# Five pairs of gates as seven block products, a hand-written ScalarE order at the border, and an earlier split of the next weights, in a bidirectional DeltaNet encoder layer

## The chip, the core and the metric

The program runs on one core of a Trainium2 chip. TensorE multiplies matrices (PE in the profile, PEld its weight loads), VectorE (DVE) and ScalarE (ACT) work on tiles, GpSimd (POOL) does small things, and SyncE's queue (SP) issues the DMAs. The metric is the device time of one execution in microseconds; 2003.53 us is the median of three runs before the change.

## What is computed

One encoder layer over 1040 positions (16 learned tokens and 1024 of the sequence), width 1024, all in float32. A normed input is projected into q, k, v, z, two sets of scalars, three parts of a short convolution and two gates:

```python
h = rmsnorm(h_res, norm1_w[l])
proj = h @ w_in[l]
(q, k, v, z, b_raw, a_raw, sc_b, sc_c, sc_x, gate_a, gate_b) = jnp.split(proj, SPLIT_POINTS, axis=-1)
o_dn = gated_deltanet_bidir(q, k, v, z, b_raw, a_raw, dn_conv_w[l], A_log[l], dt_bias[l], dn_norm_w[l])
y_a = o_dn @ w_branch_dn[l]
y_b = (sc_b * depthwise_conv_centred(sc_c * sc_x, sc_conv_w[l])) @ w_branch_sc[l]
merged = jax.nn.sigmoid(gate_a) * y_a + jax.nn.sigmoid(gate_b) * y_b
h_res = h_res + merged @ w_out[l]
...
gu = h2 @ w_gate_up[l]
h_res = h_res + (jax.nn.silu(gu[..., :D_FF]) * gu[..., D_FF:]) @ w_down[l]
```

The DeltaNet has 8 heads; each runs a scan over chunks forwards and one backwards, after the inverse of a triangular matrix for each chunk.

## The kernel before

**Precision.** Each dense product is made of three: weights and inputs are split into a high part (a cast on ACT, to `fp32r`) and a low part (the rest, a subtraction on DVE), and high·high, high·low and low·high are added in PSUM. So a weight block of 128 columns (a unit) against 512 positions is 8 x 3 = 24 matmuls of 512 columns, and its weights cost a DMA of 512 KB, a cast `wh` and a subtraction `wl`.

**Phase one** (the loop at L1377) works through units: three for each head (q, k, v: `u_qkv`) and fill units. Beside them run generators for each head: decay, norms and k·k products (`g_norm`, L603 to L642), the inverse (`g_inv`), the scan (`g_scan`, L816 to L953). The order of all engines is the program's own here (`manual_schedule`): a planner counts estimated times for PE, DVE and ACT in `T`, gives a generator a turn after each product when its due time has passed (`run_streams`), and lets queued DVE work go when DVE would be idle (`pump`). `pick` takes the next unit, head units first, and issues its DMA. The fill units are 24 of the short convolution (8 x three, `u_short`; the second of three is multiplied out of PSUM by DVE at L437), 8 gates (`u_gate`: for GH = 4 columns blocks, A and B; a tanh on ACT and a DMA) and 5 of z (`u_z`: a tanh on ACT, a multiplication on DVE, a DMA). Gates and z stand first (L965). The weights of the next unit are split by halves in four parts, at products 33, 36, 39 and 42 of the current unit (`SPL`, L1371), in the order high, low, high, low (`split_part`, L993 on ACT and L990 on DVE). A head's output is transposed on PE, copied by ACT into its own tile `NP` (L951) and written to `o_d`.

**The border** (L1483 to L1605) follows. Three z blocks are left (z0, z1, z2 in `z_rows`: for each half 24 matmuls, a tanh into `sz`, then a DVE multiplication). The four blocks of both gates that are left go in pairs: gates A and B of one column block are made by `pair` with seven block products instead of eight (`product`: 12 matmuls of 512 columns each): A11·B11, A12·B21, S2·T2, S1·T1, S3·T3, S4·B22, A22·T4. The moving blocks T1 to T4 are sums of blocks of the input, made once by `moving_sums` (subtractions and additions of 128x2048 on DVE, then `split`). The stationary blocks are sums of weight blocks for each pair (`pair_weights`, `sums`, `stationary2`). In `pair`, A11·B11 is put in the PSUM tile `bank`, ACT copies it to `o1`, and S2·T2 is added to the same `bank`. In the border DVE and PE keep the order of the text, and the other engines are ordered by the scheduler; after the first pair all are.

**Tiles.** `wh` and `wl` have two buffers each. Raw weights have two slots in phase one, and two more from L1482 on, in memory (`tp`) that phase one's tiles give back. PSUM has three kinds of bank in the profile: pm (2), pe (3), pd (3). After the border come the two branch products, the merge and the feed-forward; they are as before.

Of the kernel before, what the change touches and what calls it, by code (L numbers as in the profile page):

```python
# [16 lines left out]
P = 128  # L17
# [7 lines left out]
H = 8  # L25
# [1 line left out]
FF = 2816  # L27
NF = FF // P
ZH = 5
GH = 4  # L30
EPS = 1e-6
NEG = -1e30

# [15 lines left out]
def encoder_layer(ctx: ExitStack, tc: tile.TileContext, x, meta, norm1_w, w_in, w_ba,  # L49
                  dn_conv_w, A_log, dt_bias, dn_norm_w, sc_conv_w, w_bdn, w_bsc,  # L50
                  w_out, norm2_w, w_gu, w_down, final_w, out):
    nc = tc.nc
# [222 lines left out]
    def V(n, kind=0):  # L275
        return on("dve", (68 + 1.042 * n, 130 + 1.042 * n, 130 + 0.52 * n)[kind])

    def A(n):
        return on("act", 144 + 0.834 * n)
# [505 lines left out]
    def g_scan(h, st_):  # L785
# [74 lines left out]
        for i in range(NC):  # L860
# [12 lines left out]
            for d in act_:  # L873
# [4 lines left out]
                t = V(P, 1)  # L878
# [64 lines left out]
            yield T["pe"] + 300  # L943
        yield T["dve"] + HOP
        for c4 in range(2):
            oT = NP[:, 4 * c4:4 * c4 + 4, 1 - c4]
            pt = newbank()
            for c in range(4):
                transpose(pt[:, c], oacc[4 * c4 + c])
            yield pe(430)  # L950
            nc.scalar.copy(oT, pt)  # L951
            A(512)
            nc.sync.dma_start(o_d[h][:, c4 * 512:(c4 + 1) * 512].rearrange("p (c t) -> p c t", c=4), oT)  # L953
# [8 lines left out]
    fill_units += [(off + j * P, lambda w, j=j, d_=d_[j]: u_gate(j, d_, w), None, None)  # L962
                   for j in range(GH) for off, d_ in ((OGA, ta_d), (OGB, tb_d))]
    fill_units += [(OZ + h * P, lambda w, h=h: u_z(h, w), None, None) for h in range(ZH)]
    fill_units = fill_units[24:] + fill_units[:24]  # L965
    done = freed = 0
    decs, norms, invs, scans = [], [], [], []

# [16 lines left out]

    def split_part(u, i):
        u[3][0] = i + 1
        k = slice(4 * (i // 2), 4 * (i // 2) + 4)
        if i % 2:
            nc.vector.tensor_tensor(out=u[1][1][:, k], in0=u[2][:, k], in1=u[1][0][:, k].bitcast(F32), op=ALU.subtract)  # L990
            V(512)
        else:
            nc.scalar.copy(u[1][0][:, k], u[2][:, k])  # L993
            A(512)

    def start_streams():
        nonlocal ndec, nnorm, ninv, nscan
# [370 lines left out]
                yield T["act"]  # L1368

    dn = ph1.enter_context(tc.tile_pool(name="dn", bufs=1))  # L1370
    SPL = (33, 36, 39, 42)  # L1371
    for g in (gen0, gen1):
        for _ in g:
            pass
# [2 lines left out]
    while done < H or qkv_units or fill_units or any(ahead):  # L1377
        u = ahead.pop(0)
        if u is None:
            run_streams()  # L1380
            pump()
            T["pe"] += 100
            ahead.append(pick())
            continue
        for k in range(u[3][0], 4):
            split_part(u, k)
        if ahead[0]:
            ahead[0][1] = wtiles([P, KT, P])
        ahead.append(pick())
        for n_, _ in enumerate(u[0][1](u[1])):  # L1390
            if ahead[0] and n_ in SPL:
                split_part(ahead[0], SPL.index(n_))
            run_streams()
            pump()
    ph1.close()
# [46 lines left out]
    def moving_sums():  # L1442

        c = [slice(C0 + META + 512 * i, C0 + META + 512 * i + 512) for i in range(2)]
        f = lambda m: m.bitcast(F32)
        h0, h1 = ([f(hx[0][:, 4 * i:4 * i + 4, cc]) for cc in c] for i in range(2))
        l0, l1, l2 = ([f(t[:, :, cc]) for cc in c] for t in low_tiles)
        for i in range(2):
            for j in range(2):
                mov[f"B{i + 1}{j + 1}"] = hx[0][:, 4 * i:4 * i + 4, c[j]], [hx[1][4 * i + k][:, c[j]] for k in range(4)]  # L1450
        for i, n in enumerate(("T1", "T2", "T3")):
            t = big(f"b{i}", [P, 2, 4, 512])
            mov[n] = t[:, 0], t[:, 1]
        x, y = (big(g, [P, 2, 4, 512], F32) for g in ("mA", "b3"))
        t1, t2, t3, d_ = x[:, 0], x[:, 1], y[:, 0], y[:, 1]
        a, b = slice(0, 2), slice(2, 4)
        sub(t1, h0[1], h0[0])
        sub(d_, l0[1], l0[0])
        add(t1, t1, d_)
        split(*mov["T1"], t1)  # L1460
        yield
        sub(t2, h1[1], t1)
        add(t2[:, a], t2[:, a], l1[1])
        add(t2[:, b], t2[:, b], l2[1])
        split(*mov["T2"], t2)
        yield
        sub(t3, h1[1], h0[1])
        sub(d_[:, a], l1[1], l0[1][:, a])
        sub(d_[:, b], l2[1], l0[1][:, b])
        add(t3, t3, d_)  # L1470
        split(*mov["T3"], t3)
        yield
        t = big("b3", [P, 2, 4, 512])
        mov["T4"] = t[:, 0], t[:, 1]
        sub(t1, h1[0], t2)
        add(t1[:, a], t1[:, a], l1[0])
        add(t1[:, b], t1[:, b], l2[0])
        split(*mov["T4"], t1)
        yield

    raw_slots.extend((tp, f"raw{i}") for i in range(2))
    left, right = slice(0, 512), slice(512, 1024)  # L1482
    border0 = ExitStack()  # L1483
    border0.enter_context(tc.manual_schedule(engines={mybir.EngineType.DVE, mybir.EngineType.PE}))
    z_units = [wload(w_in, unit(OZ + ZH * P))]

    def z_rows(h):
# [93 lines left out]

    sums_of_blocks = moving_sums()
    z0, z1, z2 = (z_rows(h) for h in range(ZH, H))
    next(sums_of_blocks)
    z_units.append(wload(w_in, unit(OZ + (ZH + 1) * P)))
    next(z0)
    next(z0)
    next(sums_of_blocks)
    z_units.append(wload(w_in, unit(OZ + (H - 1) * P)))
    next(z0)  # L1590
    pair0 = pair_weights(0, GH)
    next(z1)
    pair0[1]()
    next(z1)
    pair0[2]()
    next(z1)
    next(z2)
    next(sums_of_blocks)
    next(z2)
    next(sums_of_blocks)  # L1600
    next(z2)
    for n, j in enumerate(range(GH, KT)):
        o1 = pair(n, j, *(pair_weights(n, j) if n else pair0))
        if n == 0:
            border0.close()  # L1605
# [370 lines left out]
```

## Time and profile before

| | |
|---|---|
| median of three runs | 2003.53 us (2002.02 to 2005.52) |
| the profiled execution | 2004.27 us, of it 2002.5 us from first to last instruction |
| phase one ends, z0 begins | 970.2 us |
| the first pair begins | 1009.3 us |
| TensorE matmul busy, DVE busy, ACT busy | 99%, 70%, 42% of the span |

A line of the waits names who waited, its line, for whom, then the microseconds in all, how many times, and the longest. A row of the timeline has the start in us, the length, the engine and line, what is written and read, how many, and in brackets the idle time before it and what ended it. Matmuls overlap: the length of one is no step, the distance between two starts is. A row of the windows has for each engine the busy time and the count, then the granted TensorE clock (1.00 is full), the busy share of the DMA engines and GB/s.

### The profile page before, as it was taken

The numbers are of one execution on the slowest core, as the hardware profiler recorded it, in microseconds if no ns is written. First come the engines' busy times: TensorE is split into PE (matmuls) and PEld (weight loads), VectorE is DVE, ScalarE is ACT, GpSimd is POOL, SyncE is SP. The second block draws the span as 40 slices with busy tenths as digits, with TensorE's granted clock in tenths as the row PEclk, the third lists the DMA queues.
The fourth block names the chain that finished last, engine by engine and source line by source line (L and its number), as shares of the span: only waits on it lengthen the run. The fifth ranks groups of instructions, "written<-read, shape, count | busy, mean of one in ns | idle before, by whom it ended". The sixth has DMA issues, their size and how long they took to land.

```text
span 2002.5 us, 31873 instructions
## 1 busy us (share of the span) xinstructions
PE 1977.3 (99%) x12011; PEld 1724.1 (86%) x12011; DVE 1396.6 (70%) x3013; ACT 836.4 (42%) x1961; POOL 107.8 (5%) x407
## 2 busy tenths in 40 slices
PE   9999999999999999999999999999999999999998
PEld 8998889899999999999788888887878888888887
DVE  6887688878888888855685544469766666656575
ACT  6472465536463646333244221225323333334344
POOL 2011101010101010100000000000000000000000
PEclk9999999999999999999999999999999999999999
DMA  3123222222132222221236743123765345477654
GB/s 132 65 90 95 80 80 75 85 61 83 45 99 59 75 59 75 59 65 43 95 116 242 249 160 95 63 93 110 256 217 217 123 155 188 158 273 244 195 172 167
DMA packets 131121, 251.00 MB, mean 125 GB/s; under 512 B 45013, under 2 KB 54662, under 8 KB 128535
## 3 DMA queue, kind: packets, MB, share of 16 engines
q1 hardware_dynamic: 130391, 247.92, 37.5%
q8 instruction: 94, 1.54, 0.3%
q10 hardware_dynamic: 576, 1.05, 0.1%
q14 instruction: 60, 0.49, 0.1%
HBM read 180.67 MB, written 68.25 MB: 124 GB/s over the span
## 4 chain that ended last, share of the span: by engine, by line
PE 90%; DVE 4%; DMA 3%; ACT 1%; issue 1%; SPq 0%; DVEq 0%; ACTq 0%
PE pm L341 33%; PE pd L1440 12%; PE pe L1440 5%; PE pm L1440 3%; PE pd L903 1%; PE pd L882 1%; PE pd L866 1%; PE pe L136 1%; PE pe L134 1%; PE pd L869 1%; PE pe L135 1%; PE pe L603 1%; PE pd L134 1%; PE pd L136 1%; PE pd L135 1%; PE pe L1882 1%
## 5 line engine op out<-in xcount | busy, mean ns | idle before, releaser
L341 PE MATMUL pm<-hTh,wh 128*128 128x512 f32 (+4 forms) x1296 | 446.4, 350 | 0.3 <-ACT hTh L1103 0.2
L341 PE MATMUL pm<-al,wh 128*128 128x512 f32 (+4 forms) x1296 | 445.9, 349 | 0.0
L341 PE MATMUL pm<-hTh,wl 128*128 128x512 f32 (+4 forms) x1296 | 443.8, 348 | 0.0
L341 PEld LDWEIGHTS pm<-hTh,wh 128*128 128x128 f32 x1296 | 242.7, 188 | 13.7 <-issue 0.8
L341 PEld LDWEIGHTS pm<-hTh,wl 128*128 128x128 f32 x1296 | 242.9, 188 | 12.3 <-issue 0.4
L341 PEld LDWEIGHTS pm<-al,wh 128*128 128x128 f32 x1296 | 242.9, 188 | 12.2 <-issue 0.4
L102 DVE TENSOR_TENSOR al<-raw,ring_h 128x1024 fp32r<-128x1024 f32 x73 | 88.6, 1222 | 65.0 <-ACT ring_h L101 64.7
L101 ACT CAST ring_h<-raw 128x1024 fp32r<-128x1024 f32 x73 | 76.7, 1053 | 107.8 <-PE pd L1884 34.4
L990 DVE TENSOR_TENSOR wl<-raw,wh 128x512 fp32r<-128x512 f32 x118 | 79.5, 688 | 30.6 <-ACT wh L993 30.2
L363 DVE SCALAR_TENSOR_TENSOR kq<-ra,wc,kq 128x520 f32<-128x520 f32 x128 | 96.6, 755 | 4.8 <-ACT kq L393 3.5
L889 ACT ACTIVATE w<-pd,small 128x128 f32<-128x128 f32 x128 | 39.9, 363 | 117.1 <-PE pd L882 116.7
L101 ACT CAST wh<-raw 128x1024 fp32r<-128x1024 f32 x47 | 49.3, 1050 | 87.4 <-PE pe L135 25.5
L496 DVE TENSOR_TENSOR tm<-fP,fN 128x135 f32<-128x135 f32 (+23 forms) x248 | 72.0, 290 | 4.9
L500 DVE TENSOR_TENSOR fP<-fP,tm 128x135 f32<-128x135 f32 (+23 forms) x248 | 71.6, 289 | 5.1
L993 ACT CAST wh<-raw 128x512 fp32r<-128x512 f32 x118 | 69.2, 621 | 3.7 <-issue 3.6
L1409 DVE TENSOR_TENSOR b<-pd,b 128x512 f32<-128x512 f32 x22 | 15.2, 690 | 69.4 <-PE pd L1440 69.4
L1819 ACT ACTIVATE b<-b 128x512 f32<-128x512 f32 x22 | 13.9, 632 | 114.3 <-DVE b L1409 114.3
L102 DVE TENSOR_TENSOR wl<-raw,wh 128x1024 fp32r<-128x1024 f32 x47 | 57.3, 1219 | 3.8 <-ACT wh L101 3.7
L856 ACT ACTIVATE jk<-NP 128x128 f32<-128x128 f32 x64 | 19.9, 311 | 83.5 <-DVE NP L852 82.5
L876 DVE SCALAR_TENSOR_TENSOR r<-pd,negEG,vS 128x128 f32<-128x128 f32 x120 | 36.8, 345 | 25.7 <-PE pd L866 25.2
L1440 PE MATMUL pd<-b_hl,wh 128*128 128x512 f32 x176 | 54.5, 391 | 0.0
L912 DVE SCALAR_TENSOR_TENSOR S<-S,eGl,pd 128x128 f32<-128x128 f32 x104 | 31.6, 342 | 30.2 <-PE pd L899 29.8
(590 smaller groups left out, 4689.5 us busy)
## 6 DMA issues: line engine op xcount, KB each, us to landing
raw<-in_w_in_dram SPq DMA_DIRECT2D x72, 512.0 KB
raw<-in_w_gate_up_dram SPq DMA_DIRECT2D x44, 512.0 KB
sums<-in_w_down_dram SPq DMA_DIRECT2D x22, 512.0 KB
t_d<-sums SPq DMA_DIRECT2D x11, 1024.0 KB
raw<-s_d SPq DMA_DIRECT2D x44, 256.0 KB
raw<-t_d SPq DMA_DIRECT2D x44, 256.0 KB
act_d<-b SPq DMA_DIRECT2D x43, 256.0 KB
raw<-act_d SPq DMA_DIRECT2D x33, 256.0 KB
```

Of the source, the lines that this page charges most:

```text
L101: nc.scalar.copy(hi, src)
L102: nc.vector.tensor_tensor(out=lo, in0=src, in1=hi.bitcast(F32), op=ALU.subtract)
L134: mm(po[:m, :n], wh[:, k, :m], xhk[:, t0:t0 + n], start=(k == 0), stop=False)
L135: mm(po[:m, :n], wh[:, k, :m], xlk[:, t0:t0 + n], start=False, stop=False)
L136: mm(po[:m, :n], wl[:, k, :m], xhk[:, t0:t0 + n], start=False, stop=(k == KT - 1))
L341: mm(po[:, :n], ww[:, k], f(k)[:, t0:t0 + n], start=i == 0, stop=i == 3 * KT - 1)
L363: nc.vector.scalar_tensor_tensor(out=acc, in0=raw[:, h0 + t:h0 + t + hn], scalar=wc[:, t, col:col + 1], in1=acc, op0=ALU.mult, op1=ALU.add)
L496: nc.vector.tensor_tensor(out=tv, in0=fP[:, 0:r, j:j + 1].broadcast_to([P, r, n]), in1=fN[:, j:j + 1, j + 1:32].broadcast_to([P, r, n]), o ...
L500: nc.vector.tensor_tensor(out=fP[:, 0:r, j + 1:32], in0=fP[:, 0:r, j + 1:32], in1=tv, op=ALU.subtract)
L990: nc.vector.tensor_tensor(out=u[1][1][:, k], in0=u[2][:, k], in1=u[1][0][:, k].bitcast(F32), op=ALU.subtract)
L993: nc.scalar.copy(u[1][0][:, k], u[2][:, k])
L1440: mm(po, x[:, k], y, start=k + i == 0 and not add_to, stop=k == 3 and i == 2, skip_group_check=add_to)
```

## The change

`GH` goes from 4 to 3: six gate units stay in phase one, and five pairs are made at the border. Of the fill units three gates come first, then the 24 of the short convolution, then three gates and five z. A head's output is copied into the tile of its values, `vS`, which the scan has done with, in place of `NP`. `split_part` casts both halves first, at products 24 and 27, and each low part follows from product 30 on when the planner takes its cast for done, at the latest from 44 on. At the border ACT too keeps the order of the text. There z1's weights are loaded before the first sum, `moving_sums` has its high and low parts in steps of their own, and z2's and the pair's steps stand in another order around them.

```diff
-GH = 4
+GH = 3
...
-            oT = NP[:, 4 * c4:4 * c4 + 4, 1 - c4]
+            oT = vS[:, 4 * c4:4 * c4 + 4]
...
-    fill_units = fill_units[24:] + fill_units[:24]
+    fill_units = fill_units[24:24 + 3] + fill_units[:24] + fill_units[24 + 3:]
...
-        k = slice(4 * (i // 2), 4 * (i // 2) + 4)
-        if i % 2:
+        k = slice(4 * (i % 2), 4 * (i % 2) + 4)
+        if i >= 2:
             nc.vector.tensor_tensor(out=u[1][1][:, k], in0=u[2][:, k], in1=u[1][0][:, k].bitcast(F32), op=ALU.subtract)
+            on("dve", 0, u[3][i - 1] - TOPE + HOP)
             V(512)
         else:
             nc.scalar.copy(u[1][0][:, k], u[2][:, k])
-            A(512)
+            u[3].append(A(512))
+
+    def split_due(u, n):
+
+        i = u[3][0]
+        if i < 2:
+            return n >= SPL[i]
+        return i < 4 and (n >= LATEST or n >= 30 and u[3][i - 1] - TOPE + HOP <= max(T["pe"], T["dve"]))
...
-    SPL = (33, 36, 39, 42)
+    SPL, LATEST = (24, 27), 44
...
-            if ahead[0] and n_ in SPL:
-                split_part(ahead[0], SPL.index(n_))
+            if ahead[0] and split_due(ahead[0], n_):
+                split_part(ahead[0], ahead[0][3][0])
...
+        high = lambda n, t: nc.scalar.copy(mov[n][0], t)
+        low_part = lambda n, t: sub(mov[n][1], t, f(mov[n][0]))
         sub(t1, h0[1], h0[0])
         sub(d_, l0[1], l0[0])
         add(t1, t1, d_)
-        split(*mov["T1"], t1)
+        high("T1", t1)
         yield
         sub(t2, h1[1], t1)
         add(t2[:, a], t2[:, a], l1[1])
         add(t2[:, b], t2[:, b], l2[1])
-        split(*mov["T2"], t2)
+        high("T2", t2)
+        low_part("T1", t1)
+        yield
+        low_part("T2", t2)
         yield
         sub(t3, h1[1], h0[1])
         sub(d_[:, a], l1[1], l0[1][:, a])
         sub(d_[:, b], l2[1], l0[1][:, b])
         add(t3, t3, d_)
-        split(*mov["T3"], t3)
+        high("T3", t3)
+        yield
+        sub(t1, h1[0], t2)
+        low_part("T3", t3)
         yield
         t = big("b3", [P, 2, 4, 512])
         mov["T4"] = t[:, 0], t[:, 1]
-        sub(t1, h1[0], t2)
         add(t1[:, a], t1[:, a], l1[0])
         add(t1[:, b], t1[:, b], l2[0])
-        split(*mov["T4"], t1)
+        high("T4", t1)
+        yield
+        low_part("T4", t1)
         yield
...
-    border0.enter_context(tc.manual_schedule(engines={mybir.EngineType.DVE, mybir.EngineType.PE}))
+    border0.enter_context(tc.manual_schedule(engines={mybir.EngineType.DVE, mybir.EngineType.PE, mybir.EngineType.Activation}))
...
-    next(sums_of_blocks)
     z_units.append(wload(w_in, unit(OZ + (ZH + 1) * P)))
     next(z0)
+    next(sums_of_blocks)
+    next(sums_of_blocks)
     next(z0)
+    z_units.append(wload(w_in, unit(OZ + (H - 1) * P)))
     next(sums_of_blocks)
-    z_units.append(wload(w_in, unit(OZ + (H - 1) * P)))
     next(z0)
+    next(z1)
     pair0 = pair_weights(0, GH)
     next(z1)
     pair0[1]()
     next(z1)
     pair0[2]()
-    next(z1)
     next(z2)
     next(sums_of_blocks)
     next(z2)
     next(sums_of_blocks)
+    next(sums_of_blocks)
     next(z2)
+    next(sums_of_blocks)
```

How the rows move is shown at three places; a row has the line, the operation, the tile written, the tiles read and the size. Tile numbers differ between the two programs, and so do lines (L1440 is L1448 now, L1409 is L1417, L1493 is L1510, L1495 is L1512, L1534 is L1551).

DVE at the start of the border, before: mA is the sum that becomes T1 and then T2, b_2088 is T1's tile, wl_12346 the low part of z1's weights.

```order
L451 TENSOR_TENSOR rb_12272<-pm_12293,rb_12272 128x512
L179 TENSOR_TENSOR mA_12338<-hTh 128x2048
L179 TENSOR_TENSOR b_2092_12339<-al_124 128x2048
L1409 TENSOR_TENSOR mA_12338<-mA_12338,b_2092_12339 128x2048
L102 TENSOR_TENSOR b_2088_12335<-mA_12338,b_2088_12335 128x2048
L102 TENSOR_TENSOR wl_12346<-raw_12347,wh_12345 128x1024
L1495 TENSOR_SCALAR s_2096_12351<-s_2096_12351,pm_12352 128x512
```

And now (wl_12208 is the low part of z1's weights, wl_12282 that of z2's; L478 is the last multiplication of phase one's last z unit; b_2079 is T1's tile).

```order
L102 TENSOR_TENSOR wl_12208<-raw_12209,wh_12207 128x1024
L478 TENSOR_SCALAR rb_12188<-rb_12188,pm_12143 128x512
L179 TENSOR_TENSOR mA_12243<-hTh 128x2048
L179 TENSOR_TENSOR b_2083_12244<-al_124 128x2048
L1417 TENSOR_TENSOR mA_12243<-mA_12243,b_2083_12244 128x2048
L179 TENSOR_TENSOR mA_12243<-hTh,mA_12243 128x2048
L1417 TENSOR_TENSOR mA_12243<-mA_12243,al_125 128x1024
L1417 TENSOR_TENSOR mA_12243<-mA_12243,al_126 128x1024
L179 TENSOR_TENSOR b_2079_12240<-mA_12243,b_2079_12240 128x2048
L1512 TENSOR_SCALAR s_2077_12213<-s_2077_12213,pm_12214 128x512
L102 TENSOR_TENSOR wl_12282<-raw_12283,wh_12281 128x1024
```

z1's low part has gone from behind T1 to the front; T1's low part stands behind the sum for T2.

ACT around the first pair, before: L1493 is z2's tanh, L1534 and L1546 copy the first pair's `bank` (pd_12564) to `o1`, the copies to b_2090 and b_2114 are the high parts of T3 and T4.

```order
L1493 ACTIVATE s_2111_12494<-pd_12528 128x512
L1534 COPY s_2115_12562<-pd_12564 128x512
L101 COPY wh_12787<-raw_12789 128x1024
L1546 COPY s_2115_12562<-pd_12564 128x512
L101 COPY b_2090_12337<-b_2092_12339 128x2048
L1548 COPY s_2116_12563<-pe_12593 128x512
L101 COPY b_2114_12554<-mA_12338 128x2048
```

And now (wh_12539 and wh_12659 are the high parts of the second and the third pair's weights, b_2081 and b_2100 those of T3 and T4, pd_12436 the first pair's `bank`).

```order
L1510 ACTIVATE s_2097_12366<-pd_12367 128x512
L101 COPY wh_12539<-raw_12541 128x1024
L101 COPY wh_12659<-raw_12661 128x1024
L1465 COPY b_2081_12242<-b_2083_12244 128x2048
L1510 ACTIVATE s_2097_12366<-pd_12399 128x512
L1465 COPY b_2100_12427<-mA_12243 128x2048
L1551 COPY s_2101_12434<-pd_12436 128x512
L101 COPY mA_12536<-raw_12542 128x1024
```

The first copy out of `bank` stood in front of the high parts of T3 and T4, and stands behind both.

PE in the first pair, before: pd_12564 takes S2·T2 and then the first product of S3·T3, pe_12593 S1·T1, and pe_12691 belongs to the second pair.

```order
L1440 MATMUL pm_12578<-hTh,wl_12421 128x512
L1440 MATMUL pd_12564<-b_2089_12336,mB_12418 128x512 x12
L1440 MATMUL pe_12593<-b_2088_12335,mB_12418 128x512 x12
L1440 MATMUL pd_12564<-b_2090_12337,mB_12418 128x512
L1440 MATMUL pe_12691<-hTh,wh_12667 128x512
```

And now (pd_12547 is the second pair's `bank`, with all twelve products of its A11·B11, of which the last is the first row here; pd_12667 is the third pair's).

```order
L1448 MATMUL pd_12547<-hTh,wl_12540 128x512
L1448 MATMUL pd_12667<-hTh,wh_12659 128x512
L1448 MATMUL pd_12667<-al_124,wh_12659 128x512
L1448 MATMUL pd_12436<-b_2080_12241,mB_12317 128x512 x12
L1448 MATMUL pe_12465<-b_2079_12240,mB_12317 128x512 x12
L1448 MATMUL pd_12436<-b_2081_12242,mB_12317 128x512 x12
```

Twelve products of the second pair and two of the third have come in front of S2·T2, which stood right behind A12·B21.

## The prediction

> **What bounds the kernel now.** I read the page's busy times first, then PE's waits, then the windows by stage, and then the timeline of the stage where PE waits.
>
> ```profile
> span 2002.5 us, 31873 instructions
> PE 1977.3 (99%) x12011; PEld 1724.1 (86%) x12011; DVE 1396.6 (70%) x3013; ACT 836.4 (42%) x1961; POOL 107.8 (5%) x407
> ```
>
> TensorE sets the end, so a change counts by the products it saves and by the holes it closes or opens in PE's row. The rows of PE's waits in what is changed:
>
> ```profile
> PE pe L136 <- DVE wl L102: 3.8, 1, 3.8
> PE pe L603 <- DVE PQ L642: 1.9, 1, 1.9
> ```
>
> The first is in the border, the second the longest of phase one. The windows (phase one after its start, the z blocks of the border, the first pairs, and the stretch behind the hole) have in the last columns the granted clock, the DMA share and GB/s:
>
> ```profile
> 100.00:960.00 860.00, 855.83 (x6891) 789.08 (x6890) 672.30 (x1975) 421.88 (x1373) 95.01 (x363) 1.00 0.24 73
> 970.15:1009.33 39.18, 35.35 (x146) 28.71 (x144) 28.71 (x25) 12.86 (x14) 0.00 (x0) 0.91 0.23 74
> 1009.33:1090.00 80.67, 80.67 (x355) 65.93 (x354) 57.30 (x59) 41.57 (x54) 0.00 (x0) 1.00 0.53 184
> 984.00:990.00 6.00, 4.49 (x11) 3.53 (x12) 5.96 (x6) 0.00 (x0) 0.00 (x0) 0.50 0.26 87
> ```
>
> In 860 us of phase one PE's row has 4.2 us free (860.00 - 855.83), in the pairs none. The z blocks lose. PE's rows there (the first of z0, three of z1, two as the clock comes back), and from the chain of waits twelve products of a pair:
>
> ```profile
> 970.18 0.39 PE L134 MATMUL pm<-hTh,wh 128*128 128x512 f32 x1
> 981.29 0.39 PE L135 MATMUL pe<-al,wh 128*128 128x512 f32 x1
> 985.51 0.79 PE L136 MATMUL pe<-hTh,wl 128*128 128x512 f32 x1 [3.83 <-DVE wl L102]
> 986.10 0.63 PE L134 MATMUL pe<-hTh,wh 128*128 128x512 f32 x1
> 986.53 0.63 PE L135 MATMUL pe<-al,wh 128*128 128x512 f32 x1
> 990.96 0.39 PE L134 MATMUL pe<-hTh,wh 128*128 128x512 f32 x1
> ...
> 1009.49 2.72 PE pd L1440 x12
> ```
>
> Twelve products of 512 columns take 2.72 us, 0.2267 us each. The six z halves are 144 of them, 32.64 us; they took from 970.18 to the first pair at 1009.33, 39.15 us. So the border loses 6.5 us: 4.0 while PE waits for z1's low weights (985.51 - 981.29 - 0.23), and some 2.5 behind it at a granted clock of 0.50, where products stand 0.43 us apart (986.10 to 986.53).
>
> **The change, part by part.**
>
> *Fifth pair.* Two gate units of 48 products leave phase one, and a pair of 7 x 12 = 84 comes to the border: 12 products less, **-2.72 us**. Its weight sums on DVE and its casts lie beside 19 us of products, as those of the pairs in 1009.33:1090.00 do, where DVE is busy 57.30 of 80.67 us; without that cover they would cost PE about 14 us a pair (a quarter of 57.30).
>
> *z1's weights first.* z1's cast needs its buffer, free when phase one's last product ends, and then 1.05 us of ACT; the subtraction follows at 2.4 us after z0's start, and PE asks for it at 11.1. The hole closes: **-6.5 us**, from -4.0 (the wait alone) to -6.5.
>
> *ACT in the order of the text.* This is where I expect the gain to be given back. S2·T2 is added to the bank that A11·B11 filled, so it can't begin before ACT's first copy out of it, and that copy now stands behind the high part of T4, which stands behind nearly all of DVE's border work. Rows of DVE, before:
>
> ```profile
> 970.38 0.69 DVE L451 TENSOR_TENSOR rb<-pm,rb 128x512 f32<-128x512 f32 x1 [4.70 <-PE pm L341]
> 973.24 2.29 DVE L179 TENSOR_TENSOR mA<-hTh 128x2048 f32<-128x2048 f32 x1 [2.16 <-DMA p_d<-rb]
> 975.45 2.28 DVE L179 TENSOR_TENSOR b<-al 128x2048 f32<-128x2048 f32 x1
> 977.76 2.29 DVE L1409 TENSOR_TENSOR mA<-mA,b 128x2048 f32<-128x2048 f32 x1
> 982.03 2.29 DVE L102 TENSOR_TENSOR b<-mA,b 128x2048 fp32r<-128x2048 f32 x1 [1.98 <-ACT b L101]
> 984.24 1.22 DVE L102 TENSOR_TENSOR wl<-raw,wh 128x1024 fp32r<-128x1024 f32 x1
> 985.37 0.68 DVE L1495 SCALAR_TENSOR_TENSOR s<-s,pm 128x512 f32<-128x512 f32 x1
> 985.97 2.28 DVE L179 TENSOR_TENSOR mA<-hTh,mA 128x2048 f32<-128x2048 f32 x1
> 988.29 2.36 DVE L1409 TENSOR_TENSOR mA<-mA,al 128x1024 f32<-128x1024 f32 x2
> 994.83 1.22 DVE L102 TENSOR_TENSOR wl<-raw,wh 128x1024 fp32r<-128x1024 f32 x1
> ```
>
> and of ACT (a cast of a unit's weights, a tanh of a z half, the high part of T1, a cast that waited for a DMA, the first copy out of a pair's bank):
>
> ```profile
> 970.15 1.05 ACT L101 CAST wh<-raw 128x1024 fp32r<-128x1024 f32 x1 [9.82 <-PE pm L341]
> 975.82 0.60 ACT L1493 ACTIVATE s<-pm 128x512 f32<-128x512 f32 x1 [1.99 <-PE pm L136]
> 980.09 1.91 ACT L101 CAST b<-mA 128x2048 fp32r<-128x2048 f32 x1 [3.67 <-DVE mA L1409]
> 1000.63 0.62 ACT L101 CAST u_hl<-raw 128x512 fp32r<-128x512 f32 x1 [0.62 <-DMA raw<-in_w_in_dram]
> 1012.25 0.59 ACT L1534 COPY s<-pd 128x512 f32<-128x512 f32 x1 [1.36 <-PE pd L1440]
> ```
>
> Times from here on are counted from z0's first product. The sums can't begin before the last DMA out of phase one's tiles has landed, since their tiles lie in that memory: 3.06 us before (973.24), 2.17 us after its DVE instruction ended. That instruction now follows a cast (1.05), a tanh (0.60) and z1's subtraction in the queue, so it ends near 3.0 us, and the sums start at 5.15. From there to the last addition for T4 DVE has, by start-to-start distances: ten of 128x2048 at 2.21 (982.03 to 984.24), six of them 0.1 later because they read what the one before wrote (975.45 to 977.76), 22.7; three pairs of 128x1024 at 2.36, 7.1; five single ones of 128x1024 at 1.13, 5.65; thirteen of 128x512 at 0.60, 7.8. That is 43.25 us. It waits for ACT twice: for z2's cast behind the high part of T2, 0.6, and for the cast of the first pair's sums, 1.05 + 0.1. Pair one's second raw block, whose slot z2 gives back at 21.3, comes 4.5 us later as before (996.05 to 1000.63), just in time. So the last addition ends at 5.15 + 43.25 + 1.75 = 50.15, T4's high part at 52.05, and the copy at 52.6.
>
> PE has until then 144 products of z, 24 of the first pair and the 14 of later pairs in front of S2·T2: 182 x 0.2267 = 41.25 us. It stands still for 52.65 - 41.25 = **11.4 us**. It is in three holes, since the three pd banks go to z2's halves and the first pair, and the second and third pair wait for DVE's multiplications of z2, at 43.3 and 50.7: about 5.2 us, 4.7 and 1.5. Bounds: if the sums start at 3.06 and DVE never waits for ACT, 7.55 us; with 2 us more for a late DMA, 13.4. Behind the holes the clock: the products that run at half speed between the holes cost nothing, because PE waits again, and those after the last hole cost between 0 and the 2.5 us seen now; I take 1.5, nearer the row, since the longest holes exceed its 3.83 us. Sum **+12.9 us**, from 7.5 to 15.9. Behind the copy on ACT are the casts of the second pair's sums, needed by PE only five products of twelve later; T4's low part follows on DVE at 55, needed by A22·T4 after 63.
>
> [...]
>
> *Phase one.* Less fill shifts nothing onto a bare scan: in the new order the last z unit still ends behind the last scan's products. Streams and dense products are mixed more finely; a burst between dense products costs at its two edges:
>
> ```profile
> 936.52 0.40 PE L341 MATMUL pm<-hTh,wl 128*128 128x322 f32 x1
> 936.76 0.61 PE L903 MATMUL pd<-v,PQ 128*128 128x128 f32 x4
> 937.12 0.39 PE L341 MATMUL pm<-hTh,wh 128*128 128x322 f32 x1
> 937.35 0.31 PE L341 MATMUL pm<-al,wh 128*128 128x322 f32 x1
> 937.50 0.31 PE L341 MATMUL pm<-hTh,wl 128*128 128x322 f32 x1
> ```
>
> 0.24 and 0.23 us instead of 0.15, together 0.17. The order has 420 such bursts where it had 398: 22 x 0.17 = 3.7 us if each is new, nothing if the joined bursts cost as much; I take the middle, +1.9. Casts that come earlier spare DVE waits:
>
> ```profile
> L990 DVE TENSOR_TENSOR wl<-raw,wh 128x512 fp32r<-128x512 f32 x118 | 79.5, 688 | 30.6 <-ACT wh L993 30.2
> L639 DVE SCALAR_TENSOR_TENSOR NP<-pe,small,PQ 128x128 f32<-128x128 f32 x128 | 38.6, 341 | 1.9 <-DMA o_d<-NP 1.4
> ```
>
> 30.2 us of DVE's 860, and a DVE that is less behind shortens PE's 4.2 free us; the least it can bring is nothing, the most 4.2, and DVE gets busier in the middle because the short convolutions move there. I take -1.0. The outputs in `vS` take away the 1.4 us that DVE waited for `NP`; in `vS` the next scan's first copy waits for the DMA, but a whole inverse and a z or convolution unit stand between them, so 0. Phase one: **+0.9**, from -4.2 to +5.
>
> *Sum.* Against the profiled execution's 2004.27 us (span 2002.5 and 1.8 around it): -2.72 - 6.5 + 12.9 + 0.9 = +4.6, 2008.85. That execution lies 0.74 above the median 2003.53, so the median after is **2008.1 us**.
>
> **The rivals.**
>
> *The border costs nothing.* ACT's copy is released in time, and only the closed hole shows: 2003.53 - 2.72 - 6.5 + 0.9 = 1995.2. For it: the sums have less to wait for in their new steps. Against it: DVE's 43 us are in its own queue ahead of T4's high part, and PE has only 41 us to hide them and the 5 before.
>
> *Phase one gains.* DVE without the waits for casts keeps up, and PE loses its free time: -4.2 instead of +0.9, 2003.0. For it: the 30.2 us. Against: PE waits for DVE in a few places only.
>
> *Phase one gets worse.* The short convolutions have their second product evicted by DVE (L437), and start while DVE is at its busiest; PE then waits for a pm bank or for k·k as at L603. Price: one more wait of 1.9 us in five of the eight heads, +9.5, 2017.6. It decides from the point where DVE, now busy 672.3 of 860 us, has no free time left in a head. Against it: DVE has 22% on the mean.
>
> **How the numbers follow.** Forecast 0.55 (2004.5 to 2012), border for nothing 0.12, phase one gains 0.18, phase one worse 0.15. A measurement of this kernel can tell about 0.2%, 4.0 us, from no change: faster is below 1999.5, slower above 2007.5. Faster: 0.12 and a quarter of the gains, 0.16. Same: the rest of the gains, 0.14, and 0.12 of the forecast's lower part, 0.26. Slower: 0.43 and 0.15, 0.58. The range 1999 to 2015 leaves out the free border (0.12) and half of the worse phase one (0.08), and holds the border's bounds (2002.7 to 2011.1).
>
> **What would show it.** Right: no wait of PE for z1's `wl` at L136; six z halves in 32.6 us; then waits of PE in L1448 of 7 to 14 us together, the last released by ACT's copy at L1551, itself right behind T4's cast; windows there below clock 1.00; z0 starting 20 to 22 us earlier. Wrong: S2·T2 right after the second pair's twelve products (then ACT's order doesn't bind), z0 starting over 25 us earlier or under 17 (then phase one decides), or PE waiting for the fifth pair's weights.

## The result, and the profile after

The changed kernel takes 2010.97 us (median of six runs, 2009.95 to 2013.91); the kernel before, run beside it, 2004.36 us (2001.18 to 2006.41). The ratio is 1.004, with a 95% interval from 1.003 to 1.005: slower, by 6.6 us between the medians. The profiled execution took 2012.82 us, 2011.1 of them from first to last instruction. Two executions in a slow state, one of 7923 us of the kernel before and one of 2176 us in experiment 7, are left out of all that follows.

The page of the changed kernel begins with its span and the busy times:

```profile
span 2011.1 us, 31898 instructions
...
PE 1979.6 (98%) x11999; PEld 1721.4 (86%) x11999; DVE 1394.1 (69%) x3020; ACT 837.6 (42%) x1964; POOL 118.7 (6%) x407
```

TensorE has 12 matmuls less to do, and its row is idle for longer. Where, the waits of PE tell:

```profile
PE pd L1448 <- DVE s L1512: 8.5, 2, 5.9
PE pd L1448 <- DVE b L1417: 3.0, 2, 1.9
...
PE pd L1448 <- ACT s L1551: 0.7, 1, 0.7
...
PE pd L134 <- ACT wh L101: 0.6, 1, 0.6
PE pd L136 <- DVE wl L102: 0.5, 1, 0.5
...
PE pe L603 <- DVE PQ L642: 0.5, 1, 0.5
```

The 3.8 us for z1's low weights is gone. New are 9.2 us in the pairs (8.5 and 0.7), and two short waits for z2's weights; phase one's wait at L603 fell from 1.9 to 0.5. The second line belongs to later stages.

I cut the span in three: up to z0's first product, from there to the first product of the branch (W_bsc, the first L134 behind the pairs), and the rest. The windows of before for the last two, then those of after (columns as in the prediction, the granted clock third from the end):

```profile
970.18:1086.08 115.90, 112.07 (x481) 91.39 (x480) 82.37 (x79) 52.45 (x65) 0.00 (x0) 0.97 0.41 142
1086.08:2002.55 916.47, 902.97 (x3997) 745.53 (x3995) 561.69 (x791) 308.12 (x400) 0.00 (x0) 0.99 0.52 176
```

```profile
948.92:1092.79 143.87, 133.59 (x566) 108.17 (x564) 91.33 (x90) 60.12 (x77) 0.00 (x0) 0.95 0.37 129
1092.79:2011.06 918.27, 903.46 (x3997) 745.39 (x3995) 561.88 (x791) 308.07 (x400) 0.00 (x0) 0.99 0.52 176
```

z0 starts 21.26 us earlier (948.92 against 970.18), 0.5 less than the 21.76 of the two gate units that left phase one (96 products of 0.2267). The border's 480 products would take 108.8 us without a hole, its 564 now 127.9: it lost 7.1 us before and loses 16.0 now. The rest is 1.8 us longer with the same instructions. -21.3 + 28.0 + 1.8 = 8.5 us, the difference of the spans. The medians differ by 6.6 only, since the profiled execution lies 1.9 us above its median; so these parts are those of one execution.

The rows of PE round the holes, of the changed kernel (z2's first product, its first with low weights, and the first behind z2; the last product of the first pair's B11 and B21, the second pair's first and last, the third pair's first two, S2·T2, S1·T1):

```profile
971.43 0.50 PE L134 MATMUL pd<-hTh,wh 128*128 128x512 f32 x1 [0.59 <-ACT wh L101]
972.69 0.50 PE L136 MATMUL pd<-hTh,wl 128*128 128x512 f32 x1 [0.53 <-DVE wl L102]
...
983.27 0.39 PE L1448 MATMUL pd<-hTh,wh 128*128 128x512 f32 x1
...
988.49 0.39 PE L1448 MATMUL pm<-hTh,wl 128*128 128x512 f32 x1
994.74 0.76 PE L1448 MATMUL pd<-hTh,wh 128*128 128x512 f32 x1 [5.87 <-DVE s L1512]
...
998.88 0.40 PE L1448 MATMUL pd<-hTh,wl 128*128 128x512 f32 x1
1001.93 0.79 PE L1448 MATMUL pd<-hTh,wh 128*128 128x512 f32 x1 [2.64 <-DVE s L1512]
1002.52 0.63 PE L1448 MATMUL pd<-al,wh 128*128 128x512 f32 x1
1003.80 5.08 PE L1448 MATMUL pd<-b,mB 128*128 128x512 f32 x12 [0.65 <-ACT s L1551]
1008.72 2.88 PE L1448 MATMUL pe<-b,mB 128*128 128x512 f32 x12
```

Measured from start to start, less the 0.23 us of a product, z2's weights are late by 1.4 us, and the three holes behind are 6.0, 2.8 and 1.1 us. The six z halves take 34.35 us (983.27 - 948.92), 1.7 more than their 144 products without a hole. The rows of ACT and DVE beside them:

```profile
1001.36 1.90 ACT L1465 CAST b<-mA 128x2048 fp32r<-128x2048 f32 x1 [4.93 <-DVE mA L1417]
1003.17 0.58 ACT L1551 COPY s<-pd 128x512 f32<-128x512 f32 x1
```

```profile
998.92 2.35 DVE L1417 TENSOR_TENSOR mA<-mA,al 128x1024 f32<-128x1024 f32 x2
1001.19 0.68 DVE L1512 SCALAR_TENSOR_TENSOR s<-s,pd 128x512 f32<-128x512 f32 x1
```

The bank that ACT copies at 1003.17 was full at about 986, when the pair's next products began in another bank. The copy stands behind T4's high part, which waited 4.93 us for DVE's last addition. So the third hole ends with ACT's copy; the first two end with DVE's multiplications of z2 (L1512), which stand between the sums in DVE's queue. S2·T2 starts 54.9 us after z0; 182 products without a hole would have brought it there at 41.25. Its twelve products then take 4.92 us instead of 2.72, as the windows with the granted clock show:

```profile
991.21:998.04 6.83, 3.30 (x8) 2.65 (x9) 6.83 (x5) 2.40 (x2) 0.00 (x0) 0.50 0.00 0
998.04:1001.45 3.41, 1.24 (x6) 0.67 (x4) 3.41 (x4) 0.09 (x1) 0.00 (x0) 1.00 0.00 0
1001.45:1008.28 6.83, 5.70 (x13) 4.01 (x14) 6.70 (x7) 3.87 (x4) 0.00 (x0) 0.50 0.19 77
```

All of this happens later than forecast, because the sums began later: 7.55 us after z0 instead of 5.15. SP's queue and DVE's row there:

```profile
951.24 0.33 SPq L1528 DMA_DIRECT2D raw<-in_w_in_dram  x1
951.83 0.32 SPq L480 DMA_DIRECT2D z_d<-rb  x1
```

```profile
951.12 0.68 DVE L478 SCALAR_TENSOR_TENSOR rb<-rb,pm 128x512 f32<-128x512 f32 x1
956.47 2.29 DVE L179 TENSOR_TENSOR mA<-hTh 128x2048 f32<-128x2048 f32 x1 [4.66 <-issue]
```

Phase one's last store went out 0.6 us behind a load of 512 KB (the second pair's gate weights, whose buffer had just come free), and the sums started 4.66 us behind DVE's last instruction of phase one, not 2.17.

### The profile page after: what moved, and what is told of

Same layout as the page of the kernel before. It is cut to its first block, busy times and chain, and to the rows that moved or that the text cites. A ratio compares the mean times of both kernels' runs of the same rounds, so it can differ in the third digit from the quotient of the medians.

```text
span 2011.1 us, 31898 instructions
## 1 busy us (share of the span) xinstructions
PE 1979.6 (98%) x11999; PEld 1721.4 (86%) x11999; DVE 1394.1 (69%) x3020; ACT 837.6 (42%) x1964; POOL 118.7 (6%) x407
## 3 DMA queue, kind: packets, MB, share of 16 engines
q8 instruction: 94, 1.54, 0.3%
## 4 chain that ended last, share of the span: by engine, by line
PE 44%; DVE 5%; DMA 2%; issue 1%; ACT 1%; SPq 0%; DVEq 0%; ACTq 0%
PE pd L1448 12%; PE pe L1448 5%; PE pm L1448 3%; PE pe L1904 1%; PE pe L1902 1%; PE pe L1903 1%; PE pd L1904 1%; PE pd L1902 1%; PE pd L1903 1%; PE pd L134 1%; PE pe L134 1%; PE pd L136 1%; PE pe L136 1%; PE pe L135 1%; PE pd L135 1%
## 5 line engine op out<-in xcount | busy, mean ns | idle before, releaser
L341 PE MATMUL pm<-al,wh 128*128 128x320 f32 (+4 forms) x1264 | 435.5, 350 | 0.0
L341 PE MATMUL pm<-hTh,wl 128*128 128x320 f32 (+4 forms) x1264 | 434.7, 349 | 0.0
L341 PE MATMUL pm<-hTh,wh 128*128 128x320 f32 (+4 forms) x1264 | 431.1, 346 | 0.3 <-ACT hTh L1111 0.2
L341 PEld LDWEIGHTS pm<-hTh,wh 128*128 128x128 f32 x1264 | 236.7, 188 | 12.6 <-ACT hTh L1111 0.6
L341 PEld LDWEIGHTS pm<-hTh,wl 128*128 128x128 f32 x1264 | 237.0, 188 | 11.9 <-issue 0.6
L341 PEld LDWEIGHTS pm<-al,wh 128*128 128x128 f32 x1264 | 236.9, 188 | 11.3 <-issue 0.6
L990 DVE TENSOR_TENSOR wl<-raw,wh 128x512 fp32r<-128x512 f32 x114 | 74.6, 687 | 17.4 <-ACT wh L994 17.2
L1417 DVE TENSOR_TENSOR b<-pd,b 128x512 f32<-128x512 f32 x22 | 15.2, 690 | 68.6 <-PE pd L1448 68.6
L1448 PE MATMUL pd<-b_hl,wh 128*128 128x512 f32 x176 | 54.4, 390 | 0.0
L546 ACT ACTIVATE PQ<-PQ,negG 128x128 f32<-128x128 f32 x128 | 42.5, 395 | 24.4 <-DVE PQ L541 24.3
L1448 PE MATMUL pd<-b,mB 128*128 128x512 f32 x204 | 51.3, 402 | 0.7 <-ACT s L1551 0.7
```

The costliest lines, as they stand in the source:

```text
L341: mm(po[:, :n], ww[:, k], f(k)[:, t0:t0 + n], start=i == 0, stop=i == 3 * KT - 1)
L546: nc.scalar.activation(PQ[:, c, d], PQ[:, c, d], AF.Exp, bias=negG2[:, c, hd:hd + 1])
L1448: mm(po, x[:, k], y, start=k + i == 0 and not add_to, stop=k == 3 and i == 2, skip_group_check=add_to)
```

## The experiments

Ten kernels, each with runs of the kernel before beside it (its medians there 2001.7 to 2002.8 us, so I compare ratios or differences to it).

**1. ACT out of the text's order.** In the changed kernel:

```diff
-    border0.enter_context(tc.manual_schedule(engines={mybir.EngineType.DVE, mybir.EngineType.PE, mybir.EngineType.Activation}))
+    border0.enter_context(tc.manual_schedule(engines={mybir.EngineType.DVE, mybir.EngineType.PE}))
```

> The changed kernel with one word taken out: ScalarE is no longer held to the order of the text in the border, VectorE and TensorE still are. Theory one (the border, through ScalarE's order): the first copy out of the first pair's bank is no longer behind the high part of T4's sum, so the second and third pair wait for VectorE alone and the holes of 6.0, 2.8 and 1.1 us before S2·T2 shrink; the wait at L1448 falls from the 12.2 us of the changed kernel's profile to under 5 us, and the time from 2011 to about 2001 (1998 to 2004). Theory two (phase one, with its later low parts and mixed streams, holds the loss): the border's holes are given back elsewhere and the time stays at 2008 to 2013. Theory three (VectorE's own queue sets the holes, and ScalarE is only the last of several that release them): the two larger holes, which VectorE's multiplications of z2 ended, stay, the last one of 1.1 us goes, and the time is 2009 to 2010.

1994.47 us against 2002.80 before, 0.996 [0.9948, 0.9972]: below what any theory said, and faster than both kernels. The window, and rows of ACT and PE:

```profile
947.38:1076.53 129.15, 128.58 (x566) 105.53 (x564) 91.08 (x90) 60.43 (x77) 0.00 (x0) 1.00 0.41 144
```

```profile
958.37 1.05 ACT L101 CAST wh<-raw 128x1024 fp32r<-128x1024 f32 x1 [2.43 <-DMA raw<-in_w_in_dram]
...
983.79 0.59 ACT L1551 COPY s<-pd 128x512 f32<-128x512 f32 x1 [0.94 <-PE pd L1448]
```

```profile
986.31 2.88 PE L1448 MATMUL pd<-b,mB 128*128 128x512 f32 x12
```

The border loses 1.3 us instead of 16.0, at full clock. The copy comes as soon as the bank is full; S2·T2 follows the first pair's products without a wait, 38.9 us after z0, ahead of the products that need DVE's multiplications of z2 (the scheduler orders them so once the copy is early, so PE's order changes together with ACT's). z2's cast runs at 958.37, 11 us after z0, instead of 21 (970.35 in the changed kernel, behind T2's high part). DVE's queue is the same down to T4's low part; theory three, that it makes the holes by itself, falls.

**2. The border of before in the changed kernel**, with five pairs and the new phase one:

```diff
-        high("T1", t1)
+        split(*mov["T1"], t1)
...
-    border0.enter_context(tc.manual_schedule(engines={mybir.EngineType.DVE, mybir.EngineType.PE, mybir.EngineType.Activation}))
+    border0.enter_context(tc.manual_schedule(engines={mybir.EngineType.DVE, mybir.EngineType.PE}))
...
+    next(sums_of_blocks)
     z_units.append(wload(w_in, unit(OZ + (ZH + 1) * P)))
     next(z0)
-    next(sums_of_blocks)
-    next(sums_of_blocks)
...
```

> The changed kernel with the border of before (the order of the sums' and z weights' steps, the steps' contents, ScalarE free), but with five pairs and phase one as changed. Theory one (the border loses about 9 us, phase one nothing much, the fifth pair gains 2.7): 2004.4 - 2.7 + 0.5 to 2, that is 2002 to 2004, with the wait for z1's weights of 3.8 us back and none at L1448. Theory two (phase one holds the loss): 2009 to 2012.

2002.40 us, 0.9994 [0.9986, 1.0003]: theory one by the time. Without the new border, the rest of the change does nothing that the time shows; but the wait for z1's weights, forecast at 3.8 us, is 5.7 (experiment 6 shows where that comes from).

**3. The new border in the kernel before**, the same hunks the other way round.

> The kernel before with the changed border alone (four pairs and phase one as before). Theory one: the border's loss without the fifth pair's gain, 2004.4 + 7 to 10, that is 2011 to 2014, with PE waits at L1448 of 8 to 13 us. Theory two (phase one holds the loss): 2000 to 2005.

2008.88 us, 1.0033 [1.0021, 1.0045]: theory one, a little under its numbers. The stretch from z0 to the branch takes 120.69 us for 480 products, 11.9 lost; PE waits 5.9 us for z2's multiplications. Experiments 2 and 3 together put the loss in the border.

**4. z1's weights first, alone**, in the kernel before:

```diff
+    z_units.append(wload(w_in, unit(OZ + (ZH + 1) * P)))
     next(sums_of_blocks)
-    z_units.append(wload(w_in, unit(OZ + (ZH + 1) * P)))
     next(z0)
```

> The kernel before with one step moved: z1's weights are split in front of the first of the sums' steps, nothing else. Theory one: the hole of 3.83 us before z1 goes and with it the stretch at half clock, and nothing else comes late: 2004.4 - 4 to 6.5, that is 1998 to 2000.5, and the stretch from z0 to the first branch product falls from 115.9 to about 110 us. Rival: the sums, each about 3 us later, now hold S1·T1's or S2·T2's products, and the hole comes back there: 2003 to 2006.

2000.10 us, 0.9986 [0.9977, 0.9994]. The hole before z1 is gone, but only 2.2 of 7.1 us came back in the stretch (113.68, where theory one had about 110). The time lies in theory one's range (1998 to 2000.5) and not in the rival's. Yet the rival was right that a hole comes back, though wrong on the place; it is at z2's low weights:

```profile
PE pd L136 <- DVE wl L102: 2.4, 1, 2.4
```

**5. The copy first, with ACT in the text's order.** In the changed kernel (the last hunk stands in `pair`, which gets `behind` for the first pair alone):

```diff
-    next(sums_of_blocks)
...
-    next(sums_of_blocks)
-    next(sums_of_blocks)
-    next(z2)
-    next(sums_of_blocks)
+    behind = (z2, sums_of_blocks, sums_of_blocks, sums_of_blocks, sums_of_blocks)
...
             nc.scalar.copy(o1[:, left], bank)
+            for step in behind:
+                next(step)
```

> The changed kernel with ScalarE still held to the text's order, but the last z half, T3's and T4's steps written behind the first copy out of the first pair's bank, so that the copy no longer follows T4's high part. Theory one (that copy's place in ScalarE's queue makes the holes): S2·T2 follows the first pair's dense products without a wait, the holes of 6.0, 2.8 and 1.1 us and the half clock behind them go, and what stays is the late weights of z2 (1.4 us) and perhaps a wait of S3·T3 for its sums (0 to 4 us): 1996 to 2002. Theory two (the gain of freeing ScalarE came from its casts of weights and its tanh, which keep their late places here): over 2005.

2000.81 us, 0.9985 [0.9976, 0.9994]: in theory one's range. Rows of PE:

```profile
988.02 2.88 PE L1448 MATMUL pd<-b,mB 128*128 128x512 f32 x12
...
1002.98 0.50 PE L1448 MATMUL pd<-hTh,wl 128*128 128x512 f32 x1 [3.01 <-DVE wl L102]
```

S2·T2 starts 39.7 us after z0, without a wait. The border still loses 6.9 us (134.72 for 564 products): z2's weights are late by 1.4 as before, and the third pair's low weights stand, as in the changed kernel, behind T4's additions in DVE's queue; PE now gets there early enough to wait for them, 3.0 us with slower products behind (a granted clock of 0.65 in 1002.98:1007.90). The three holes go, though z2's cast keeps its late place on ACT. But the edit moves more than the copy: z2's two multiplications, which ended the first two holes, now also stand in front of T3's sum on DVE:

```profile
985.43 1.27 DVE L1512 SCALAR_TENSOR_TENSOR s<-s,pd 128x512 f32<-128x512 f32 x2
```

where the changed kernel has them at 993.92 and 1001.19. So this run doesn't show what the copy's place is worth alone.

**6. Phase one alone**, in the kernel before:

```diff
-            oT = NP[:, 4 * c4:4 * c4 + 4, 1 - c4]
+            oT = vS[:, 4 * c4:4 * c4 + 4]
...
-    fill_units = fill_units[24:] + fill_units[:24]
+    fill_units = fill_units[24:24 + 3] + fill_units[:24] + fill_units[24 + 3:]
...
-    SPL = (33, 36, 39, 42)
+    SPL, LATEST = (24, 27), 44
...
-            if ahead[0] and n_ in SPL:
-                split_part(ahead[0], SPL.index(n_))
+            if ahead[0] and split_due(ahead[0], n_):
+                split_part(ahead[0], ahead[0][3][0])
```

> The kernel before with the edits of phase one alone: high parts at products 24 and 27 and low parts when due, three units of gates first, scan outputs from the tile of values; four pairs and the border as before. Theory one (phase one is nearly free, from z0's start of 948.92 us, 0.5 us behind what the two missing units would give): 2003 to 2006. Theory two (phase one loses several us, hidden in the stages that follow): over 2007. Theory three (it gains, since VectorE's waits for casts fall from 30.2 to 17.4 us): under 2002.

2002.90 us, 0.9999 [0.9990, 1.0008], beside 2002.79: nothing by the time, which is next to theory one's range (2003 to 2006). The profile shows two effects that nearly cancel up to z0, which starts at 969.84 instead of 970.18. The windows up to there, before and here:

```profile
0.00:970.18 970.18, 962.27 (x7535) 887.16 (x7536) 752.53 (x2144) 475.79 (x1497) 107.77 (x407) 1.00 0.25 76
0.00:969.84 969.84, 963.30 (x7536) 885.10 (x7537) 743.66 (x2144) 473.81 (x1496) 116.63 (x407) 1.00 0.24 76
```

PE's row is free for 6.5 us instead of 7.9, and busy for 1.0 longer with the same products. DVE's waits for casts of weights fell from 30.2 us, here to 22.3 and in the changed kernel (114 of these instructions, not 118) to 17.2:

```profile
L990 DVE TENSOR_TENSOR wl<-raw,wh 128x512 fp32r<-128x512 f32 x118 | 77.2, 686 | 22.6 <-ACT wh L994 22.3
```

For the most part that idle time was not TensorE's. And the border gets worse: phase one now ends with a unit of z, whose last multiplication waits for a tanh, so the sums start 4.5 us after z0 (974.31 - 969.84) instead of 3.1, and the hole before z1, 3.8 us before, grows by 1.9, 1.4 of it from this:

```profile
PE pe L136 <- DVE wl L102: 5.7, 1, 5.7
```

The stretch from z0 to the branch loses 9.4 us (118.20 for 480 products) instead of 7.1. That the time is the same all the same is due to the rest, 913.13 us here and 916.47 in the profile of before.

**7. One transfer later.** In the changed kernel, the second pair's first load waits for T1's high part:

```diff
         rg, ru = (rawtile([P, KT, P]) for _ in range(2))
+        if n == 1:
+            nc.gpsimd.tensor_copy(rg[:, 0, 0:1], mov["T1"][0][:, 0, 0:1].bitcast(F32))
```

> The changed kernel with one transfer moved: the second pair's first 512 KB of raw weights, issued 0.6 us in front of phase one's last store to z_d, now waits (by a write of one column by GpSimd) for the high part of T1, and goes out behind that store. All other instructions keep their order. Theory one (the store landed 4.6 us after its issue instead of some 2 because of that transfer, and the sums start behind it): the sums start 5 us after z0 instead of 7.55, all that follows them on VectorE moves by the same, S2·T2 starts 2 to 2.5 us earlier and the time is 2007 to 2009.5. Theory two (the store is slow for another reason, or the holes don't follow the start of the sums): 2010 to 2012.

2006.19 us, 1.0017 [1.0008, 1.0026], where the changed kernel has 1.004. Rows of DVE, ACT and PE:

```profile
950.34 0.68 DVE L478 SCALAR_TENSOR_TENSOR rb<-rb,pm 128x512 f32<-128x512 f32 x1
953.16 2.29 DVE L179 TENSOR_TENSOR mA<-hTh 128x2048 f32<-128x2048 f32 x1 [2.14 <-DMA z_d<-rb]
```

```profile
999.86 0.58 ACT L1553 COPY s<-pd 128x512 f32<-128x512 f32 x1
```

```profile
1000.49 5.49 PE L1448 MATMUL pd<-b,mB 128*128 128x512 f32 x12 [1.14 <-ACT s L1553]
```

The store lands 2.14 us behind DVE, the sums start 5.0 us after z0 (953.16 - 948.14), and S2·T2 52.35 instead of 54.9. Theory one by the mechanism; the time lies a little below its range (2007 to 2009.5). z2's weights are in time too: the first pair begins at 980.78, the six z halves take 32.64 us. The border gained less than S2·T2 did, 1.7 us (142.13), since S2·T2 and S1·T1 run slower here (a granted clock of 0.50 from 999.74 to 1006.6) and lose some 3 us; the rest of the program was 3.6 us shorter with the same instructions in the same order, of which more below.

**8. Four pairs with ACT free**: experiment 1 with `GH = 4` in place of 3.

> The kernel with ScalarE free (the first experiment, 1994.5 us) with four pairs instead of five. Theory one (the fifth pair saves twelve products of 0.2267 us, 2.72 us, once the border has no holes): 1996.5 to 1998. Theory two (the fifth pair brings nothing, since in the border of before it brought 0.4 us): 1994 to 1995.5.

1994.69 us, 0.9958 [0.9945, 0.9970]: theory two by the median, though the two intervals are too wide to exclude 2.7 us. In the two profiles the fifth pair's gain is there up to the branch, at 1080.04 here and 1076.53 in experiment 1, and partly given back later: the rest takes 912.94 us here and 914.98 there. Among PE's waits of experiment 1 stands

```profile
PE pd L1448 <- DVE b L1417: 2.3, 2, 1.6
```

its longest at 1485.9; this kernel has no wait on that line. But the number of pairs isn't shown to be the cause: the kernel before and experiments 3, 4, 6 and 10, all with four pairs, have 0.8 to 2.2 us there (their line is L1409 or L1417). The rest takes 912.94 to 916.47 us in the six profiles with four pairs and 914.63 to 918.56 in the six with five, so the ranges overlap.

**9. Experiments 1 and 7 together.**

> The first and the seventh experiment together: five pairs, ScalarE free, and the second pair's first raw weights issued behind phase one's last store. Theory one (with ScalarE free the sums are no longer what TensorE waits for: the stretch from z0 to the first branch product lost only 1.3 us): the sums start 2.4 us earlier and nothing else changes, 1993 to 1995. Theory two (the earlier sums help what follows too, as in the seventh experiment, where the time fell by 4.5 us and the border by 1.7): 1989 to 1992.

1994.33 us, 0.9963 [0.9950, 0.9976]: theory one. The sums start 5.0 us after z0, the border loses 0.2 us (128.09), and the time is that of experiment 1. With ACT free, the start of the sums matters little: in experiment 1 z2's low weights, which stand behind them on DVE, come 0.6 us late, and here they are in time.

**10. The new border with ACT free in the kernel before**: experiment 3 without `Activation`.

> The kernel before (four pairs, phase one of before) with the changed order of the border, and ScalarE free in it. It differs from the eighth experiment (1994.7 us) in phase one alone. Theory one (the edits of phase one are worth nothing, as in the sixth experiment): 1993.5 to 1996.5. Theory two (they gain something that the hole in the border hid in the sixth experiment): 1997 to 2000. In both cases the changed order of the border gains 6 to 9 us on the kernel before once ScalarE isn't held to the text, and the loss in the changed kernel came from that one word.

1995.75 us, 0.9970 [0.9960, 0.9981]: theory one. The border takes 109.24 us for 480 products, 0.4 lost. It differs from experiment 3 in one word, and that word is worth some 13 us (0.9970 against 1.0033).

## Why the prediction was right

The forecast was 2008.1 us, slower; measured were 2010.97, and the gain of the new order was given back by ACT's copy as forecast. Part by part, the profiles give -2.7 for the fifth pair's products, +8.9 in the border (forecast -6.5 + 12.9 = +6.4), +0.5 in phase one (+0.9) and +1.8 in the rest (nothing): 8.5 against a forecast of 4.6. That the median is off by less, 2.9 us, is luck in part: the profiled execution, to which the parts belong, was 1.9 us above it.

*Fifth pair, -2.72.* Right up to the branch (3.5 us earlier in experiment 1 than in 8), but no run shows it in the whole time: by the ratios, five pairs against four cost 0.4 us with ACT free (experiments 1 and 8) and gain 1.0 in the border of before (2 and 6), neither clear of the noise.

*z1's weights first, -6.5.* The wait is gone as forecast, and experiment 10 shows the stretch nearly without loss. By itself the step is worth 2.2 us there (experiment 4), because the hole moves to z2's weights. In the changed kernel the step's worth can't be seen, since S2·T2 waits for something later anyway. One of the signs that I had named failed there: the six z halves took 34.35 us, not 32.6, because z2's cast stands behind T2's high part, which waits for the sums; with the sums in time (experiment 7) they took 32.64.

*ACT in the order of the text, +12.9.* The mechanism is shown: with the order taken away all comes back (experiments 1 and 10), in experiment 1 with DVE's queue unchanged. How much of it is the copy and how much the other late places on ACT isn't separated, since experiment 5 moves DVE's multiplications too. The size was low: S2·T2 came 13.6 us late instead of 11.4, and its slow products cost 2.2 instead of 1.5, together 15.8. The term that was too small is the landing of phase one's last store, taken as 2.17 us from the profile of before: there no load went out ahead of it. With the load out of its way (experiment 7) the sums started at 5.0 us (forecast 5.15) and S2·T2 at 52.35 (52.65), so the 43 us count of DVE's queue held: in the changed kernel 44.8 us lie between the first sum's start and the last addition's end (956.47 to 1001.27), forecast 45.0 with the waits. My bound allowed for a store 2 us late; it was 2.4.

*The clock.* The 1.5 us for slow products behind the last hole were my estimate from one case, the hole of 3.83 us before z1 with 0.50 behind it. S2·T2 did run at 0.50, but not because of the last hole: the clock was at 0.50 from 1001.45 on, inside the hole of 2.8 us and before that of 1.1. In the 3.41 us before the fall (998.04:1001.45) PE was busy for 1.24. In experiment 7 it was busy for 1.10 of the 3.41 us before the clock fell, at 999.74, inside the last hole; the hole before was 1.9 us by its row:

```profile
996.33:999.74 3.41, 1.10 (x4) 0.30 (x2) 3.41 (x5) 1.69 (x1) 0.00 (x0) 1.00 0.10 40
999.74:1003.15 3.41, 2.66 (x6) 2.15 (x7) 3.41 (x4) 1.31 (x3) 0.00 (x0) 0.50 0.28 114
```

*Phase one, +0.9.* z0 came 0.5 us later than two missing units make. Experiment 6 has both signs of the forecast up to z0, PE's row 1.4 us less free and 1.0 us longer busy, where I had taken -1.0 and +1.9; that the casts and the bursts make them isn't shown, and 1.4 us is also what the one wait at L603 fell by.

*The rest.* I counted nothing behind the pairs; the profile has 1.8 us there. With the same instructions this part took 912.94 to 918.56 us in the twelve kernels, each profiled once, so I can't say that the change makes the 1.8.

The three rivals are out: the border was not free, and experiment 6 excludes that phase one gains 4 us or loses 9.

## What to carry to other kernels

Holding an engine to the text's order turns each late operand on it into a wait for all that is written behind it (here the border lost 16.0 us with ACT held to it and 1.3 without): ask for every instruction that releases a buffer (a copy out of a bank) what stands in front of it in its queue, and who fills that. When a step is moved ahead, look one step further for the next late operand; z1's weights first only moved the hole to z2 (3.8 us before z1, then 2.4 at z2's low weights). A transfer that starts as soon as its buffer comes free can go out just ahead of a store that the next stage waits for (here 0.6 us ahead, and the sums began 4.66 us behind DVE's last instruction instead of 2.14 in experiment 7), so count the queue's other entries into its landing.

## What the runs showed of the hardware

In the changed kernel the clock fell behind a hole as short as 2.0 us (near 1500). The changes of the granted clock lie on a grid of 3.41 us (991.21, 998.04, 1001.45, 1008.28), and of two holes near 1500, of 2.0 and 2.33 us, the shorter has half clock behind it and the longer has not. The slice in front of a halved one, and the halved one, far behind the border in the changed kernel:

```profile
1499.75:1503.16 3.41, 1.54 (x7) 0.98 (x6) 3.04 (x5) 0.00 (x0) 0.00 (x0) 1.00 0.08 34
1503.16:1506.57 3.41, 3.41 (x10) 2.64 (x9) 0.92 (x2) 0.63 (x1) 0.00 (x0) 0.51 0.88 351
```

and a slice of the grid in experiment 3 (changes at 1011.3, 1018.1, 1021.5 and 1024.9), behind which the clock stayed at 1.00, though its hole was 2.33 us long, 0.3 longer than the other:

```profile
1499.36:1502.77 3.41, 1.66 (x7) 1.40 (x8) 2.68 (x5) 0.63 (x1) 0.00 (x0) 1.00 0.46 192
```

With PE busy for 1.54 of 3.41 us the next slice was halved, with 1.66 it was not; with 1.24 (998.04:1001.45 above) and 1.10 (experiment 7) it was, and so in the kernel before with 1.29 (980.39:983.80), inside its hole before z1. These are a few cases, not a measured threshold. The clock is one reason why the part behind the pairs, with the same instructions, took 914.6 us in experiment 7 and 918.3 in the changed kernel: the hole near 1500 was 1.6 us there and halved nothing, here 2.0 and it did, and the twelve products behind it took 4.45 us instead of 2.85. What sets the length of that hole (none to 2.9 us among these kernels) stays open.
